# Accumulations of the modulation rows tied behind the latest low part of the weights in VectorE's order

## The chip, the cores and the metric

The kernel runs on one core of one Trainium2 chip. The metric is the device time of one execution in microseconds, less is better. A core has TensorE (PE, matrix products), VectorE (DVE), ScalarE (ACT), GpSimd (POOL) and SyncE (SP), which here issues most of the loads; each has its own queue of instructions.

## The reference, cut to what matters

One decoder layer on 512 tokens of width 2048, in float32. A vector `c` gives six modulation rows; a normalised and modulated input goes through one wide projection, whose columns feed eight heads of dilated attention and eight heads of a gated linear recurrence; then an output projection and a squared-ReLU MLP.

```python
mod = silu(c) @ w_ada + b_ada                      # 2048 x 12288
shift1, scale1, gate1, shift2, scale2, gate2 = split(mod, 6)
h = rms_norm(x, norm1_w) * (1 + scale1) + shift1
proj = h @ w_in                                    # 2048 x 7168
aq, ak, av, gq, gf, gi, gg = split(proj)
attn = rms_norm(dilated_attention(rope(norm(aq)), rope(norm(ak)), av))
hg = rms_norm(hgrn2(gq, gf, gi)) * silu(gg)        # 8 heads, 128 channels each
x = x + gate1 * (concat(attn, hg) @ w_out)
h2 = rms_norm(x, norm2_w) * (1 + scale2) + shift2
out = x + gate2 * (square(relu(h2 @ w_ff1)) @ w_ff2)
```

## The kernel before, in words

**Weights in two parts.** Every weight tile is loaded in float32 (`wraw`, 512 KB for two tiles of 128 rows, four buffers, line 192) and split by `_split` (lines 35 to 41): ScalarE casts the high part `whi` (line 39), VectorE subtracts it from the weight to get the low part `wlo` (line 40). TensorE then takes three products per block of tokens: high by high, low by high, high by low (lines 201 to 203, and 209 to 211 where channels lie on the partitions). Both parts have four buffers, so ScalarE can cast a tile only once TensorE is done with the tile four back.

**Modulation on VectorE.** A row of the modulation is a product of a vector with a 2048-row matrix. `gemv` loads 128 rows of 512 columns at a time (`araw`, 256 KB, four buffers, line 125) and VectorE multiplies and adds them into two accumulators `acc` (line 129 for the first of each, line 131 for the others). `to_cols` adds the two (line 145), TensorE transposes the sum into a bank `pc` (line 151) and ScalarE adds over the partitions (line 154). With `early` the generator belongs to the head of the program; the others, in a list `later`, are the shift's part of the columns 4608 to 5119 of the projection (the second half of the forget gates, summed with `s1c`), gate1, scale2 and shift2, and gate2 during the output projection (summed with `sc`).

**What sets the order.** A projection steps the `later` generators by 1.85 steps for every 128 rows, between its own products; the heads' generators are stepped in the same loop. Weight loads and splits are written under high priority, so that they may run ahead. TensorE's order from line 849 on is written out as the program calls it. On VectorE, ScalarE and SP the framework's scheduler picks the order from priorities and its own estimate of times; each engine then runs its list strictly in that order.

**The recurrent heads.** For each of eight heads VectorE forms nine levels of a tile `z` (lines 607 to 617; `z` of line 609 takes the keys, of line 610 the queries, `Sx` and `f` are running products), and TensorE visits them five times: pA (levels 1, 2 and 4), pB, pC, pD (level 128, line 670) and pE. Results of pA and pB come back to VectorE through masks `mt` (line 624), `near` and `AT` (line 656). The queries of the attention are normalised by `qk_norm`: VectorE line 214, a power on GpSimd (line 215), and VectorE line 433, a factor.

## Time and profile before

| what | value |
|---|---|
| runs | 2276.13, 2276.0, 2270.74 us; median 2276.0 |
| the profiled execution | 2273.58 us, of it span 2271.7 |
| granted TensorE clock, mean | 0.997 |
| VectorE: accumulations (line 131) | 392 times, 252.9 us |
| VectorE: low parts (line 40) | 368 times, 242.7 us |
| loads of `araw` | 384 of 256 KB, 4.3 us from issue to landing |
| loads of `wraw` of the projection | 104 of 512 KB, 4.2 us |

In the rows of the profile stand the line, the engine, the operation and the tiles written and read; "<-" in brackets names what ended the idle time before. The time of a matmul is modelled; from the start of one 128x512 product to that of the next it is 0.227 us where nothing waits. The program lies in three stretches: up to 100 us modulation and the first weights, then projection and heads, and from about 1030 us on the MLP, in which no accumulation of the modulation is left.

### The profile page before, as it was taken

What the parts mean: (1) busy time and instruction counts of PE and PEld (TensorE: products, weight loads), DVE (VectorE), ACT (ScalarE), POOL (GpSimd) and SP (SyncE); (2) the same over time, 40 slices, a digit from 0 to 9 for tenths busy, and PEclk for the clock granted to TensorE, in tenths of its full rate; (3) what the DMA queues carried; (4) which work ended last, traced back from release to release, by engine and by line L of the source; (5) the groups of instructions that cost most, each with busy time, mean ns of one, the idle gap of its engine ahead of it and who ended that gap; (6) DMA issues with size and microseconds to landing.
All of it is one profiled execution on the core that took longest, in us unless ns stands there. A gap on an engine that the chain in (4) does not pass through costs nothing.

```text
span 2271.7 us, 33093 instructions
## 1 busy us (share of the span) xinstructions
PE 2212.9 (97%) x11769; PEld 1822.9 (80%) x11769; DVE 1808.1 (80%) x2765; ACT 1098.1 (48%) x1950; POOL 451.6 (20%) x664
## 2 busy tenths in 40 slices
PE   4899999999999999999999999999999999999999
PEld 3788887888778888888887888888888888888887
DVE  6999878678786575678658988998897779967878
ACT  5555444434354564457545555565564333443332
POOL 1000022000230000003232323323232222222221
PEclk9999999999999999999999999999999999999999
DMA  9799455646555266837879789889889987998884
GB/s 325 254 334 336 140 177 156 217 148 204 169 166 176 67 225 205 274 115 269 317 285 360 277 303 385 297 292 369 326 293 372 359 316 258 348 348 311 306 294 163
DMA packets 262582, 598.31 MB, mean 263 GB/s; under 512 B 23220, under 2 KB 43968, under 8 KB 262416
## 3 DMA queue, kind: packets, MB, share of 16 engines
q1 hardware_dynamic: 186800, 332.54, 43.5%
q0 software_dynamic: 70720, 254.21, 30.3%
q10 hardware_dynamic: 4896, 9.44, 1.2%
q8 instruction: 93, 1.52, 0.3%
q14 instruction: 73, 0.60, 0.1%
HBM read 518.49 MB, written 77.61 MB: 262 GB/s over the span
## 4 chain that ended last, share of the span: by engine, by line
PE 69%; DVE 11%; DMA 10%; issue 6%; POOL 2%; ACT 2%; SPq 0%; DVEq 0%; POOLq 0%; ACTq 0%
PE f L1196 10%; PE f L1197 10%; PE f L1195 10%; PE prj L201 7%; PE prj L202 6%; PE prj L203 6%; DMA araw<-in_w_ada_dram 4%; PE f L211 2%; PE f L209 2%; PE f L210 2%; DVE vlo L1180 2%; DMA f_lod<-fs 2%; DVE acc L131 2%; PE prj L210 2%; PE prj L209 2%
## 5 line engine op out<-in xcount | busy, mean ns | idle before, releaser
L1179 ACT CAST vhi<-raw 128x1024 fp32r<-128x1024 f32 x392 | 413.4, 1055 | 534.6 <-PE f L1197 416.1
L1180 DVE TENSOR_TENSOR vlo<-raw,vhi 128x1024 fp32r<-128x1024 f32 x392 | 475.8, 1219 | 151.7 <-ACT vhi L1179 151.0
L1196 PE MATMUL f<-vlo,Fh 128*128 128x512 f32 x1376 | 537.0, 390 | 3.4 <-DVE vlo L1180 3.3
L1197 PE MATMUL f<-vhi,Fl 128*128 128x512 f32 x1376 | 535.6, 389 | 1.3 <-DMA Fl<-f_lod 1.3
L1195 PE MATMUL f<-vhi,Fh 128*128 128x512 f32 x1376 | 536.0, 390 | 0.0
L39 ACT CAST whi<-wraw 128x512 fp32r<-128x512 f32 (+1 forms) x368 | 219.9, 601 | 434.9 <-PE prj L203 275.8
L201 PE MATMUL prj<-whi,hi 128*128 128x512 f32 x896 | 360.5, 402 | 2.0 <-ACT gg L711 1.3
L202 PE MATMUL prj<-wlo,hi 128*128 128x512 f32 x896 | 350.6, 391 | 2.1 <-DVE wlo L40 2.1
L203 PE MATMUL prj<-whi,lo 128*128 128x512 f32 x896 | 350.9, 392 | 0.0
L131 DVE SCALAR_TENSOR_TENSOR acc<-araw,sc,acc 128x512 f32<-128x512 f32 (+1 forms) x392 | 252.9, 672 | 102.7 <-DMA araw<-in_w_ada_dram 101.4
L40 DVE TENSOR_TENSOR wlo<-wraw,whi 128x512 fp32r<-128x512 f32 (+1 forms) x368 | 242.7, 665 | 111.3 <-ACT whi L39 108.8
L1196 PEld LDWEIGHTS f<-vlo,Fh 128*128 128x128 f32 x1376 | 258.3, 188 | 61.7 <-DVE vlo L1180 8.6
L1197 PEld LDWEIGHTS f<-vhi,Fl 128*128 128x128 f32 x1376 | 258.4, 188 | 55.0 <-DMA Fl<-f_lod 1.7
L1195 PEld LDWEIGHTS f<-vhi,Fh 128*128 128x128 f32 x1376 | 258.3, 188 | 53.7 <-issue 0.3
L1163 DVE TENSOR_TENSOR raw<-raw,raw 128x1024 f32<-128x1024 f32 x224 | 268.0, 1216 | 3.8 <-DMA raw<-in_w_ff_dram 3.3
L201 PEld LDWEIGHTS prj<-whi,hi 128*128 128x128 f32 x896 | 168.8, 188 | 37.7 <-ACT gg L711 2.1
L202 PEld LDWEIGHTS prj<-wlo,hi 128*128 128x128 f32 x896 | 168.9, 188 | 36.9 <-DVE wlo L40 4.2
L203 PEld LDWEIGHTS prj<-whi,lo 128*128 128x128 f32 x896 | 168.6, 188 | 36.6 <-DVE lo L243 0.3
L1141 POOL DMA_DIRECT2D Fh<-f_hid x112 | 79.0, 705 | 421.6 <-PE f L1197 403.0
L211 PE MATMUL f<-hi,wlo 128*128 128x512 f32 x256 | 100.0, 390 | 1.5 <-DVE wlo L40 1.5
L209 PE MATMUL f<-hi,whi 128*128 128x512 f32 x256 | 100.3, 392 | 0.0
L210 PE MATMUL f<-lo,whi 128*128 128x512 f32 x256 | 99.6, 389 | 0.0
(311 smaller groups left out, 2911.2 us busy)
## 6 DMA issues: line engine op xcount, KB each, us to landing
raw<-in_w_ff_dram SPq DMA_DIRECT2D x224, 512.0 KB, 10.3
araw<-in_w_ada_dram SPq DMA_DIRECT2D x384, 256.0 KB, 4.3
Fh<-f_hid POOLq DMA_DIRECT2D x112, 512.0 KB, 6.6
Fl<-f_lod POOLq DMA_DIRECT2D x112, 512.0 KB, 7.9
wraw<-in_w_in_dram SPq DMA_DIRECT2D x104, 512.0 KB, 4.2
Fh<-h_hid POOLq DMA_DIRECT2D x60, 512.0 KB, 5.8
Fl<-h_lod POOLq DMA_DIRECT2D x60, 512.0 KB, 7.0
f_hid<-part POOLq DMA_DIRECT2D x48, 512.0 KB, 8.0
```

Source lines behind the costliest of these rows:

```text
L39: nc.scalar.copy(hi, src)
L40: (eng or nc.vector).tensor_tensor(lo, src, hi.bitcast(F32), op=ALU.subtract)
L131: dve.scalar_tensor_tensor(acc, raw[:, k - k0], vec[:, k:k + 1], acc, op0=ALU.mult, op1=ALU.add)
L201: pe.matmul(banks[ti], lhsT=hi[:, ts], rhs=whi, start=first, stop=False)
L202: pe.matmul(banks[ti], lhsT=hi[:, ts], rhs=wlo, start=False, stop=False)
L203: pe.matmul(banks[ti], lhsT=lo[:, ts], rhs=whi, start=False, stop=last)
L1163: dve.tensor_tensor(dst, a, b, op=ALU.subtract)
L1179: cast_done.append(act.copy(hi, src))
L1180: split_done.append(dve.tensor_tensor(lo, src, hi.bitcast(F32), op=ALU.subtract))
L1195: pe.matmul(banks[t], lhsT=fh[u][a][:, ts], rhs=whi[:, a], start=first, stop=False)
L1196: pe.matmul(banks[t], lhsT=fh[u][a][:, ts], rhs=wlo[:, a], start=False, stop=False)
L1197: pe.matmul(banks[t], lhsT=fl[u][a][:, ts], rhs=whi[:, a], start=False, stop=end)
```

## The change

`_split` keeps the latest subtraction that was written, and every accumulation of a `gemv` that is not `early` is written under an edge to it. The edge orders the two on VectorE's queue; it is no semaphore and no engine waits longer for it than its queue asks.

```diff
@@ _split
-    (eng or nc.vector).tensor_tensor(lo, src, hi.bitcast(F32), op=ALU.subtract)
+    _split.low = (eng or nc.vector).tensor_tensor(lo, src, hi.bitcast(F32), op=ALU.subtract)
@@ gemv
                 acc = accs[k % 2]
-                if k < 2:
-                    dve.tensor_scalar(acc, raw[:, k - k0], vec[:, k:k + 1], None, op0=ALU.mult)
-                else:
-                    dve.scalar_tensor_tensor(acc, raw[:, k - k0], vec[:, k:k + 1], acc, op0=ALU.mult, op1=ALU.add)
+                with ExitStack() if early else tc.issue_after(_split.low.ins):
+                    if k < 2:
+                        dve.tensor_scalar(acc, raw[:, k - k0], vec[:, k:k + 1], None, op0=ALU.mult)
+                    else:
+                        dve.scalar_tensor_tensor(acc, raw[:, k - k0], vec[:, k:k + 1], acc, op0=ALU.mult, op1=ALU.add)
```

The same instructions are issued on every engine. Lines below 127 have a number one higher in the changed kernel (L132 there is L131 here). VectorE's order differs from about 135 us to the output projection, SP's in the loads that go with it, TensorE's only in about 30 places ahead of the first head.

First place, VectorE in the first recurrent head, about 240 us: the low parts `wlo`, the query activations `gq` (line 764) and the levels `z_2574` and `z_2607`, which with `z_2551` feed the visit pA. Before:

```order
L764 SCALAR_TENSOR_TENSOR gq_1302<-gq_1302,scol_2484,sg_2500 128x512
L761 TENSOR_SCALAR scol_2484<-scol_2484 128x1
L617 TENSOR_TENSOR f_1292<-f_1292 128x256
L764 SCALAR_TENSOR_TENSOR gq_2095<-gq_2095,scol_2484,sg_2504 128x512
L40 TENSOR_TENSOR wlo_2709<-wraw_2706,whi_2708 128x512
L610 TENSOR_TENSOR z_2574<-gq_1300,f_1292 128x128x2
L616 TENSOR_TENSOR Sx_2549<-Sx_2549,f_1292 128x128x2
L764 SCALAR_TENSOR_TENSOR gq_2097<-gq_2097,scol_2484,sg_2508 128x512
L617 TENSOR_TENSOR f_1292<-f_1292 128x128x2
L609 TENSOR_TENSOR z_2607<-kk_2547,Sx_2549 128x64x4
L40 TENSOR_TENSOR wlo_2713<-wraw_2706,whi_2712 128x512
L610 TENSOR_TENSOR z_2607<-gq_1300,f_1292 128x64x4
```

With the change, from `wlo_2592` on:

```order
L40 TENSOR_TENSOR wlo_2592<-wraw_2585,whi_2591 128x512
L132 SCALAR_TENSOR_TENSOR acc_2558<-araw_2612,s1c_112,acc_2558 128x512
L132 SCALAR_TENSOR_TENSOR acc_2557<-araw_2615,s1c_112,acc_2557 128x512
L762 TENSOR_SCALAR scol_2484<-scol_2484 128x1 x3
L132 SCALAR_TENSOR_TENSOR acc_2558<-araw_2700,s1c_112,acc_2558 128x512
L132 SCALAR_TENSOR_TENSOR acc_2557<-araw_2703,s1c_112,acc_2557 128x512
L765 SCALAR_TENSOR_TENSOR gq_1300<-gq_1300,scol_2484,sg_2496 128x512
L765 SCALAR_TENSOR_TENSOR gq_1302<-gq_1302,scol_2484,sg_2500 128x512
L762 TENSOR_SCALAR scol_2484<-scol_2484 128x1
L40 TENSOR_TENSOR wlo_2709<-wraw_2706,whi_2708 128x512
```

then `z_2551` (line 610), an activation `gq`, `wlo_2713`, two accumulations, an `f` and an activation `gq`, and:

```order
L40 TENSOR_TENSOR wlo_2772<-wraw_2769,whi_2771 128x512
L132 SCALAR_TENSOR_TENSOR acc_2558<-araw_2763,s1c_112,acc_2558 128x512
L132 SCALAR_TENSOR_TENSOR acc_2557<-araw_2766,s1c_112,acc_2557 128x512
L611 TENSOR_TENSOR z_2574<-gq_1300,f_1292 128x128x2
L617 TENSOR_TENSOR Sx_2549<-Sx_2549,f_1292 128x128x2
L40 TENSOR_TENSOR wlo_2776<-wraw_2769,whi_2775 128x512
L132 SCALAR_TENSOR_TENSOR acc_2558<-araw_2829,s1c_112,acc_2558 128x512
L132 SCALAR_TENSOR_TENSOR acc_2557<-araw_2857,s1c_112,acc_2557 128x512
L618 TENSOR_TENSOR f_1292<-f_1292 128x128x2
L610 TENSOR_TENSOR z_2607<-kk_2547,Sx_2549 128x64x4
L132 SCALAR_TENSOR_TENSOR acc_2558<-araw_2860,s1c_112,acc_2558 128x512
L611 TENSOR_TENSOR z_2607<-gq_1300,f_1292 128x64x4
```

The accumulations of `acc_2557` and `acc_2558` stood far ahead of this place before, in rows of 138 to 208 us; eleven of them now stand between `wlo_2592` and the end of `z_2607`.

Second place, VectorE at the third projection of the heads, about 366 us: accumulations `acc_4126` and `acc_4127` of one modulation block, and the low parts `wlo_4137` and `wlo_4141`. Before:

```order
L131 SCALAR_TENSOR_TENSOR acc_4126<-araw_4409,sc_86,acc_4126 128x512
L617 TENSOR_TENSOR f_1298<-f_1298 128x64x4
L609 TENSOR_TENSOR z_4244<-kk_4091,Sx_4093 128x32x8
L40 TENSOR_TENSOR wlo_4137<-wraw_4134,whi_4136 128x512
L131 SCALAR_TENSOR_TENSOR acc_4127<-araw_4457,sc_86,acc_4127 128x512
L131 SCALAR_TENSOR_TENSOR acc_4126<-araw_4460,sc_86,acc_4126 128x512
L610 TENSOR_TENSOR z_4244<-gq_2097,f_1298 128x32x8
L616 TENSOR_TENSOR Sx_4093<-Sx_4093,f_1298 128x32x8
L131 SCALAR_TENSOR_TENSOR acc_4127<-araw_4475,sc_86,acc_4127 128x512
L617 TENSOR_TENSOR f_1298<-f_1298 128x32x8
L145 TENSOR_TENSOR acc_4126<-acc_4126,acc_4127 128x512
L40 TENSOR_TENSOR wlo_4141<-wraw_4134,whi_4140 128x512
```

With the change:

```order
L40 TENSOR_TENSOR wlo_4075<-wraw_4068,whi_4074 128x512
L618 TENSOR_TENSOR f_1298<-f_1298 128x32x8
L130 TENSOR_SCALAR acc_4126<-araw_4128,sc_86 128x512
L170 TENSOR_TENSOR gcol_115<-gcol_115,bcol_84 128x4
L130 TENSOR_SCALAR acc_4127<-araw_4131,sc_86 128x512
L40 TENSOR_TENSOR wlo_4137<-wraw_4134,whi_4136 128x512
L40 TENSOR_TENSOR wlo_4141<-wraw_4134,whi_4140 128x512
L132 SCALAR_TENSOR_TENSOR acc_4126<-araw_4161,sc_86,acc_4126 128x512
L132 SCALAR_TENSOR_TENSOR acc_4127<-araw_4164,sc_86,acc_4127 128x512
```

The whole block but its first two products now stands behind `wlo_4141`; before, its sum (line 145) stood ahead of it.

Third place, VectorE in the sixth head, about 584 us: the factor of `qk_norm` (line 433, `rs0_6312`), which waits for GpSimd's power, and the level `z_6502`, which feeds pD. Before:

```order
L616 TENSOR_TENSOR Sx_6149<-Sx_6149,f_2089 128x4x64
L40 TENSOR_TENSOR wlo_6520<-wraw_6513,whi_6519 128x512
L617 TENSOR_TENSOR f_2089<-f_2089 128x4x64
L433 TENSOR_SCALAR rs0_6312<-rs0_6312 128x16
L40 TENSOR_TENSOR wlo_6587<-wraw_6584,whi_6586 128x512
L624 TENSOR_TENSOR mt_6494<-pB_6438,hgm_107 128x128
L609 TENSOR_TENSOR z_6502<-kk_6147,Sx_6149 128x2x128
L610 TENSOR_TENSOR z_6502<-gq_5072,f_2089 128x2x128
```

With the change:

```order
L610 TENSOR_TENSOR z_6471<-kk_6147,Sx_6149 128x4x64
L434 TENSOR_SCALAR rs0_6312<-rs0_6312 128x16
L146 TENSOR_TENSOR acc_6053<-acc_6053,acc_6054 128x512
L40 TENSOR_TENSOR wlo_6587<-wraw_6584,whi_6586 128x512
L611 TENSOR_TENSOR z_6471<-gq_5072,f_2089 128x4x64
L625 TENSOR_TENSOR mt_6494<-pB_6438,hgm_107 128x128 x2
L617 TENSOR_TENSOR Sx_6149<-Sx_6149,f_2089 128x4x64
L654 TENSOR_TENSOR near_6150<-near_6150,mt_6494 128x128
L618 TENSOR_TENSOR f_2089<-f_2089 128x4x64
L610 TENSOR_TENSOR z_6502<-kk_6147,Sx_6149 128x2x128
L657 TENSOR_TENSOR AT1_459<-near_6150,mt_6494 32x4x32 x4
L611 TENSOR_TENSOR z_6502<-gq_5072,f_2089 128x2x128
```

Line 433 (434) has moved up by half a level, and ten rows instead of four now stand between it and the end of `z_6502`.

## The prediction

> **What bounds the kernel now.** I read the page's busy times first, then the windows of 50 us, then what TensorE waited for, and last the timelines around those waits.

> ```profile
> span 2271.7 us, 33093 instructions
> PE 2212.9 (97%) x11769; PEld 1822.9 (80%) x11769; DVE 1808.1 (80%) x2765; ACT 1098.1 (48%) x1950; POOL 451.6 (20%) x664
> ```

> TensorE is busy for 97% of the span, so an edit that adds and removes no instruction can win only the idle 58.8 us (2271.7 less 2212.9). The windows tell where these lie (columns: stretch, its length, busy time and count of each engine, granted clock, DMA share, GB/s).

> ```profile
> 0.00:50.00 50.00, 20.08 (x108) 16.75 (x109) 31.61 (x84) 27.17 (x67) 9.63 (x24) 1.00 0.98 323
> 50.00:100.00 50.00, 42.17 (x180) 32.86 (x180) 50.00 (x127) 26.77 (x62) 0.00 (x0) 0.93 0.96 317
> 150.00:200.00 50.00, 49.99 (x223) 40.64 (x222) 50.00 (x88) 26.97 (x60) 0.53 (x1) 1.00 1.03 371
> 200.00:250.00 50.00, 49.46 (x346) 40.58 (x345) 46.77 (x93) 27.43 (x62) 0.00 (x0) 1.00 0.68 223
> 350.00:400.00 50.00, 48.98 (x439) 40.09 (x438) 39.66 (x87) 20.67 (x58) 9.47 (x12) 1.00 0.59 180
> 550.00:600.00 50.00, 46.45 (x421) 38.20 (x420) 39.37 (x93) 19.79 (x71) 16.59 (x26) 0.97 0.52 160
> ```

> The first 100 us hold 37.7 of the 58.8 (29.9 and 7.8), before the order of any engine differs. From 100 us on 21 us are left in all. Between 100 and 1030 us, where the tied accumulations run, TensorE waited for:

> ```profile
> PE pD L670 <- DVE z L610: 3.4, 2, 2.9
> PE prj L202 <- DVE wlo L40: 2.1, 3, 0.7
> PE f L211 <- DVE wlo L40: 1.5, 2, 0.9
> PE prj L201 <- ACT gg L711: 1.3, 1, 1.3
> PE prj L201 <- ACT whi L39: 0.6, 2, 0.3
> PE pB L583 <- DVE z L610: 0.6, 1, 0.6
> PE pc L151 <- DVE acc L145: 0.5, 1, 0.5
> ```

> That is 10.0 us. Two rows are not VectorE's late low parts or z: `gg` (1.3), and `f L211` (1.5), a projection of the MLP. The target is 7.2 us: one wait of 2.9 and a handful of 0.3 to 0.7.

> **What makes a low part late.** VectorE is 80% busy and takes its queue in order. Around 367 us (start, length, engine, line, operation, names, in brackets the idle time before):

> ```profile
> 364.87 0.75 DVE L131 SCALAR_TENSOR_TENSOR acc<-araw,sc,acc 128x512 f32<-128x512 f32 x1 [0.41 <-DMA araw<-in_w_ada_dram]
> 365.54 0.42 DVE L617 TENSOR_TENSOR f<-f 128x256 f32<-128x256 f32 x1
> 365.88 0.69 DVE L145 TENSOR_TENSOR acc<-acc 128x512 f32<-128x512 f32 x1
> 366.48 0.68 DVE L40 TENSOR_TENSOR wlo<-wraw,whi 128x512 fp32r<-128x512 f32 x1
> ...
> 367.22 0.50 PE L202 MATMUL prj<-wlo,hi 128*128 128x512 f32 x1 [0.72 <-DVE wlo L40]
> ```

> The low part did not wait for its high part; it stood behind accumulations, one of which waited for its load. TensorE started 0.06 us after the low part's end.

> **Term 1, the small waits: 3.7 us won.** In the order rows of the second place four accumulations (0.67 apart) and a sum (0.6) stood ahead of `wlo_4141`, 3.3 us; now two plain products (0.41 each) do, 2.5 us less for a wait of 0.72. The other small waits (the row of `prj L202`, that of `pB`, the lesser of the two `pD` waits, the sum `pc`) have the same make-up. Their sum is 2.1 + 0.6 + 0.5 + 0.5 = 3.7. Bounds: nothing, if the accumulations that stay ahead wait for loads as the one at 364.87 did, and 4.3 with the two waits on whi.

> **Term 2, the long wait at 586 us: 2.2 won, between 0 and 4.5.**

> ```profile
> 573.68 0.75 DVE L131 SCALAR_TENSOR_TENSOR acc<-araw,sc,acc 128x512 f32<-128x512 f32 x1 [2.00 <-DMA araw<-in_w_ada_dram]
> ...
> 577.96 0.17 DVE L214 TENSOR_SCALAR rs<-rs 128x16 f32<-128x16 f32 x1
> ...
> 584.48 0.17 DVE L433 TENSOR_SCALAR rs<-rs 128x16 f32<-128x16 f32 x1 [2.81 <-POOL rs L215]
> ...
> 585.70 0.42 DVE L610 TENSOR_TENSOR z<-gq,f 128x256 f32<-128x256 f32 x1
> ...
> 578.21 6.24 POOL L215 TENSOR_TENSOR rs<-rs,mhalf 128x16 f32<-128x16 f32 x1 [4.38 <-DVE rs L214]
> ...
> 586.26 0.68 PE L670 MATMUL pD<-z 128*128 128x128 f32 x4 [2.87 <-DVE z L610]
> ...
> 588.28 0.63 PE L202 MATMUL prj<-wlo,hi 128*128 128x512 f32 x1
> 588.71 0.63 PE L203 MATMUL prj<-whi,lo 128*128 128x512 f32 x1
> ```

> Here no accumulation is the last cause: L433 waited 2.81 us for GpSimd's power, and the z for pD stood behind L433. After the wait eight matmuls started 0.43 us apart, where the usual distance is 0.227: 8 x 0.2 = 1.6 us more, which makes the place worth 2.9 + 1.6 = 4.5. The change starts the chain earlier: the masks and L214 stood behind an accumulation that waited 2.00 us for a load, and now lie behind a low part with the accumulations after it. Against it, two accumulations (1.3 us) come between that low part and L214, and behind L433 now stand ten rows up to the end of the z: a sum and a low part (0.6 each), seven of 0.2 to 0.34 (1.9) and the four AT (1.2), with the last z 0.4, in all 4.8 us, where 1.6 stood (584.48 to 586.12). With a power of 6.24 us the z ends 11.3 us behind L214 (0.25 + 6.24 + 4.8); TensorE wants it at 583.39, so L214 must start by 572.1, 5.9 us earlier than now, for the wait to vanish. It gains the 2.00 and some of the accumulations' work ahead. I take half of the place, 2.2.

> Another run of the same power took

> ```profile
> 296.47 3.49 POOL L215 TENSOR_TENSOR rs<-rs,mhalf 128x16 f32<-128x16 f32 x1 [0.78 <-DVE rs L214]
> ```

> beside a VectorE that was just as full, so 3 us of the 6.24 may be chance. [...]

> **Term 3, the first head: 4.0 us lost, with a slow clock 5.6.** The order rows of the first place speak against the change. Before, 14 accumulations of the fifth shift group ran far ahead, at 138 to 208 us, in pairs like these:

> ```profile
> 176.69 1.40 DVE L131 SCALAR_TENSOR_TENSOR acc<-araw,s1c,acc 128x512 f32<-128x512 f32 x2
> 178.01 1.40 DVE L131 SCALAR_TENSOR_TENSOR acc<-araw,sc,acc 128x512 f32<-128x512 f32 x2
> ```

> A pair takes 1.33 us, one 0.67. Tied, they stand at 230 to 262 us, 11 of them between `wlo_2592` and the end of `z_2607`, which TensorE's first visit pA needs. The timelines of VectorE and TensorE there:

> ```profile
> 235.53 0.69 DVE L40 TENSOR_TENSOR wlo<-wraw,whi 128x512 fp32r<-128x512 f32 x1 [0.69 <-ACT whi L39]
> ...
> 238.13 0.74 DVE L764 SCALAR_TENSOR_TENSOR gq<-gq,scol,sg 128x512 f32<-128x512 f32 x1
> ...
> 243.06 0.42 DVE L610 TENSOR_TENSOR z<-gq,f 128x256 f32<-128x256 f32 x1
> 243.40 0.42 DVE L616 TENSOR_TENSOR Sx<-Sx,f 128x256 f32<-128x256 f32 x1
> ...
> 246.40 0.46 PE L583 MATMUL pA<-gq,kk 128*32 128x32 f32 x32
> 246.68 1.05 PE L583 MATMUL pA<-z 128*32 128x32 f32 x96
> ```

> The low part at 235.53 starts when its high part is cast, and these casts follow TensorE, so it can't come earlier. From its start VectorE has, by the new order: five low parts at 0.60 (3.0), 11 accumulations at 0.67 (7.3), four L764 at 0.67 (2.7), four short L761 at 0.08 (0.3), seven of z, Sx and f at 0.34 (2.3). Sum 15.6: the z ends at 251.2, where it ended at 243.48. The last third of pA's 96 matmuls starts at about 247.2 (246.68 and two thirds of its 0.8). So TensorE waits 4.0 us where it had 3.7 to spare. The eight slow matmuls of 588 us followed an idle stretch of 2.87, so another 1.6 is likely. I take 5.0, between 4.0 and 5.6.

> [...]

> **Smaller terms.** At 387 us the new order puts a sum and a low part's followers ahead of the last z for pD:

> ```profile
> 383.50 1.28 DVE L40 TENSOR_TENSOR wlo<-wraw,whi 128x512 fp32r<-128x512 f32 x2
> ...
> 385.24 0.41 DVE L610 TENSOR_TENSOR z<-gq,f 128x256 f32<-128x256 f32 x1
> ...
> 387.05 0.49 PE L670 MATMUL pD<-z 128*128 128x128 f32 x2
> ```

> The second low part starts at 384.10; behind it come itself and the sum (0.6 each), four of 0.34 and three of 0.2, then the z ends: 3.2 us later, 387.3 against 387.05. With the same at one more head I take 0.8 lost, between 0 and 2.5. The sums L145 for the transposes pc come later in the new order; TensorE waited for such a sum only once, 0.5 us, with the next work of its group far off, so I take nothing, and a late one would cost its lateness once. A wait of 1.43 us for a stage-2 low part at 1266 us sits where a VectorE row or two also moved: 0.7 won, between 0 and 1.4.

> **Sum.** -3.7 - 2.2 + 5.0 + 0.8 - 0.7 = -0.8 us. The profiled execution took 2273.58 us (span 2271.7 and 1.9 around it), so 2272.8; the median of the runs shown, 2276.0, lies 2.4 above that execution. I predict 2275.

> **The rivals.**

> *All waits cured, nothing new* (faster). The sum would be -3.7 - 4.5 - 1.4 = -9.6: 2266. For it: every low part from 140 to 970 us has less VectorE work ahead than before. Against it: term 3, which is a plain count of rows. It needs z_2607 on time, 7.7 us earlier than counted.

> *The ties make VectorE wait for loads in front of the z* (slower). The place is the first head again. The accumulation loads have four buffers, so a pair's load starts when the pair two ahead is done, and lands late:

> ```profile
> araw<-in_w_ada_dram SPq DMA_DIRECT2D x384, 256.0 KB, 4.3
> DVE acc L131 <- DMA araw<-in_w_ada_dram: 98.7, 72, 5.5
> ```

> With 4.3 to land, 0.7 for two issues and 1.33 for the pair, two pairs take 6.3 us or 3.2 each; my count spaces them 2.8 apart, so 0.4 x 5 = 2 us more. On SP's queue these loads now also stand behind weight loads that wait for a buffer; if each of five pairs waits 2.0 us, as at 573.68, the first head costs 5.6 + 10 = 15.6, terms 1 and 2 shrink to 3.7, and the time is +12 or 2288. It decides from 1.0 us a pair (5.6 + 5 x 1.0 - 3.7 is the 6.8 of the bound below). Against it: SP reached the loads of 236 to 262 us early before.

> *Term 3 absorbed, all else as summed*: -5.8, 2270, still within 0.3% of the median.

> **How the numbers follow.** The measurement tells 0.3% (6.8 us) from no change. The forecast, with its own range of 2269 to 2281 (the bounds above, -7 to +5), has 0.50; the absorbed term 3 has 0.13, three quarters of it inside 0.3%; the full cure 0.20, mostly below 2269.2; the waits for loads 0.17, nearly all above 2282.8. With the edges of the forecast, faster 0.24, same 0.59, slower 0.17, and the range that leaves out 2 in 10 is 2265 to 2284.

> **What would show it.** Term 1: the rows `prj L202 <- wlo` and `pc <- acc` gone or under 1 us in all. Term 2: the wait for L433 under 2.8 and the 550 to 600 window above 46.45. Term 3: a wait of pA for z at about 247 us, which no row shows now, with slow matmuls after it. If pA doesn't wait, the forecast is wrong toward faster; if the accumulations ahead of `z_2607` show idle time for araw, toward slower.

## The result

| kernel | median, us | lowest to highest | ratio to before, 95% interval |
|---|---|---|---|
| before | 2275.97 (11 runs) | 2270.74 to 2277.51 | |
| with the ties | 2270.97 (11 runs) | 2268.63 to 2273.67 | 0.998, 0.997 to 0.9989 |

The change wins 5.0 us, 0.22%: the interval of the ratio leaves out 1, and the gain is inside the 0.3% that was called no change. The forecast was 2275 in 2265 to 2284. Its place and sign of each large term were right; the sum was 4 us too slow. The profiled execution of the changed kernel took 2268.98 us, 4.6 less than that of before. In the changed kernel's profile all lines below 127 have a number one higher. Its totals and what TensorE waited for from 100 to 1030 us:

```profile
span 2267.1 us, 33088 instructions
PE 2212.1 (98%) x11769; PEld 1824.7 (80%) x11769; DVE 1808.9 (80%) x2765; ACT 1097.5 (48%) x1950; POOL 439.1 (19%) x664
```

```profile
PE pA L584 <- DVE z L611: 4.4, 2, 3.5
PE pho L692 <- ACT far_sb L684: 1.9, 2, 1.0
PE prj L202 <- ACT gg L712: 1.7, 2, 1.3
PE f L212 <- DVE wlo L40: 1.0, 2, 0.8
PE pD L671 <- DVE z L611: 0.9, 1, 0.9
```

The busy times of TensorE, VectorE and ScalarE changed by less than 1 us (GpSimd's fell by 12.5, from 451.6); TensorE waits elsewhere. All rows of before for projection low parts, for pB and for pc are gone, pD fell from 3.4 to 0.9, and a wait of 4.4 at pA is new, as term 3 said. What VectorE waited for turned round in the same stretch:

```profile
DVE wlo L40 <- ACT whi L39: 139.1, 97, 5.9
DVE acc L132 <- DMA araw<-in_w_ada_dram: 19.9, 22, 2.5
```

Before, accumulations waited 98.7 us for loads with low parts behind them; now low parts wait for their high part, which costs nobody anything, and most loads have landed by the time an accumulation's turn comes.

**Where the time went.** For each stretch I compared the start of the same matmul in both traces, counted from the span's start (negative: the changed kernel is earlier); below this is called matched matmuls. The sum at a time, and what each step added (rounded; drifts of 0.1 to 0.2 between the steps are left out):

| us of before | step, us | changed kernel earlier or later, us | what stands there |
|---|---|---|---|
| to 225 | -1.2 | -1.2 | the first 100 us, -0.6, and a step of -0.6 at 200 |
| 235 | -0.8 | -2.0 | wait of pc for a sum gone |
| 245 to 260 | +7.0 | +5.0 | pA, first head |
| 300 to 360 | +1.5 | +6.5 | new waits of pD and of pho (less the lesser wait of pD, gone) |
| 367 | -1.6 | +4.9 | wait for wlo gone |
| 577 | -1.2 | +3.5 | wait for wlo gone |
| 586 to 591 | -4.5 | -1.0 | pD and the slow matmuls gone |
| 620 to 655 | -1.3 | -2.3 | pB and wlo gone (-2.3), new wait of pho (+1.0) |
| to 1240 | -0.5 | -2.8 | small steps of both signs |
| 1250 to 1270 | -1.1 | -3.9 | wait of 1.4 for a stage-2 low part gone |
| to the end | -0.3 | -4.2 | |

**The first head.** VectorE and TensorE in the changed kernel around the new wait:

```profile
234.32 0.69 DVE L40 TENSOR_TENSOR wlo<-wraw,whi 128x512 fp32r<-128x512 f32 x1 [2.52 <-ACT whi L39]
234.93 1.41 DVE L132 SCALAR_TENSOR_TENSOR acc<-araw,s1c,acc 128x512 f32<-128x512 f32 x2
...
249.54 0.42 DVE L611 TENSOR_TENSOR z<-gq,f 128x256 f32<-128x256 f32 x1
...
244.44 0.46 PE L584 MATMUL pA<-gq,kk 128*32 128x32 f32 x32
244.72 0.49 PE L584 MATMUL pA<-z 128*32 128x32 f32 x32
246.08 0.46 PE L584 MATMUL pA<-z 128*32 128x32 f32 x32 [0.87 <-DVE z L611]
250.02 0.66 PE L584 MATMUL pA<-z 128*32 128x32 f32 x32 [3.48 <-DVE z L611]
250.60 0.80 PE L202 MATMUL prj<-whi,hi 128*128 128x512 f32 x1
251.20 0.63 PE L203 MATMUL prj<-wlo,hi 128*128 128x512 f32 x1
...
254.61 0.60 PE L202 MATMUL prj<-whi,hi 128*128 128x512 f32 x1
```

From the start of that low part to the end of the z are 249.96 - 234.32 = 15.6 us, the number that the count of rows gave. None of the accumulations between waited for a load. Behind the wait stand ten matmuls about 0.43 us apart.

**586 us.** The factor (line 434) waits 0.2 us instead of 2.81, and the last z ends 0.2 us before pD:

```profile
576.85 0.29 DVE L215 TENSOR_SCALAR rs<-rs 128x16 f32<-128x16 f32 x1
...
581.80 0.17 DVE L434 TENSOR_SCALAR rs<-rs 128x16 f32<-128x16 f32 x1 [0.18 <-POOL rs L216]
...
586.22 0.42 DVE L611 TENSOR_TENSOR z<-gq,f 128x256 f32<-128x256 f32 x1
...
578.81 2.95 POOL L216 TENSOR_TENSOR rs<-rs,mhalf 128x16 f32<-128x16 f32 x1
...
586.81 0.71 PE L671 MATMUL pD<-z 128*128 128x128 f32 x4
```

The way from L434 to the end of the z is 4.8 us, as counted; the power took 2.95 us instead of 6.24.

### The profile page after: what moved, and what is told of

The parts are those of the page before. It is cut to its first block, busy times and chain, and to the rows that moved or that the text cites. A ratio compares the mean times of both kernels' runs of the same rounds, so it can differ in the third digit from the quotient of the medians.

```text
span 2267.1 us, 33088 instructions
## 1 busy us (share of the span) xinstructions
PE 2212.1 (98%) x11769; PEld 1824.7 (80%) x11769; DVE 1808.9 (80%) x2765; ACT 1097.5 (48%) x1950; POOL 439.1 (19%) x664
## 4 chain that ended last, share of the span: by engine, by line
PE 67%; issue 12%; DMA 9%; DVE 8%; POOL 3%; ACT 1%; SPq 0%; POOLq 0%; DVEq 0%; ACTq 0%
PE f L1198 8%; PE f L1197 8%; PE f L1196 8%; PE prj L202 8%; PE prj L204 8%; PE prj L203 8%; DMA f_lod<-fs 2%; PE f L212 2%; PE f L210 2%; PE f L211 2%; PE prj L211 2%; PE prj L212 2%; PE prj L210 2%; DVE vlo L1181 2%; DMA Fl<-h_lod 2%
## 5 line engine op out<-in xcount | busy, mean ns | idle before, releaser
L39 ACT CAST whi<-wraw 128x512 fp32r<-128x512 f32 (+1 forms) x368 | 220.7, 602 | 464.8 <-PE prj L204 330.9
L40 DVE TENSOR_TENSOR wlo<-wraw,whi 128x512 fp32r<-128x512 f32 (+1 forms) x368 | 245.7, 671 | 181.8 <-ACT whi L39 170.5
L202 PE MATMUL prj<-whi,hi 128*128 128x512 f32 x896 | 360.7, 403 | 1.8 <-ACT gg L712 1.7
L203 PE MATMUL prj<-wlo,hi 128*128 128x512 f32 x896 | 349.8, 390 | 0.0
L132 DVE SCALAR_TENSOR_TENSOR acc<-araw,sc,acc 128x512 f32<-128x512 f32 (+1 forms) x392 | 250.4, 677 | 22.9 <-DMA araw<-in_w_ada_dram 22.2
L202 PEld LDWEIGHTS prj<-whi,hi 128*128 128x128 f32 x896 | 168.9, 189 | 36.6 <-ACT gg L712 2.9
L203 PEld LDWEIGHTS prj<-wlo,hi 128*128 128x128 f32 x896 | 169.1, 189 | 32.7
L211 PE MATMUL f<-lo,whi 128*128 128x512 f32 x256 | 99.6, 389 | 0.0
## 6 DMA issues: line engine op xcount, KB each, us to landing
araw<-in_w_ada_dram SPq DMA_DIRECT2D x384, 256.0 KB, 4.6
```

The lines of the kernel that those rows point to most:

```text
L39: nc.scalar.copy(hi, src)
L40: _split.low = (eng or nc.vector).tensor_tensor(lo, src, hi.bitcast(F32), op=ALU.subtract)
L132: dve.scalar_tensor_tensor(acc, raw[:, k - k0], vec[:, k:k + 1], acc, op0=ALU.mult, op1=ALU.add)
L202: pe.matmul(banks[ti], lhsT=hi[:, ts], rhs=whi, start=first, stop=False)
L203: pe.matmul(banks[ti], lhsT=hi[:, ts], rhs=wlo, start=False, stop=False)
```

## The experiments

Before took 2273.33 to 2274.71 us as a median beside these runs and 2275.97 in the result, so each kernel is read by its ratio to before on its own chip.

| kernel | median, us | before there | ratio, 95% interval |
|---|---|---|---|
| the change, again | 2270.95 | 2273.58 | 0.9988, 0.9979 to 0.9996 |
| the change, shift group free | 2267.31 and 2267.34 | 2273.89 and 2273.58 | 0.9969, 0.9958 to 0.9979; 0.9975, 0.9964 to 0.9985 |
| ties in the shift group alone | 2279.07 and 2279.66 | 2273.89 and 2274.71 | 1.0019, 1.001 to 1.0028; 1.0016, 1.0005 to 1.0027 |
| shift group tied from the sixth accumulation | 2267.71 | 2273.58 | 0.9974, 0.9965 to 0.9984 |
| before, factor on GpSimd | 2269.4 | 2273.89 | 0.9987, 0.9978 to 0.9996 |
| shift group free, factor on GpSimd | 2266.55 | 2273.58 | 0.9967, 0.9955 to 0.9979 |
| ties in gate2 alone | 2274.5 | 2274.71 | 0.9999, 0.9991 to 1.0008 |
| shift group free, ties one pair looser | 2263.94 | 2274.71 | 0.9956, 0.9943 to 0.997 |
| shift group free, ties two pairs looser | 2263.28 | 2273.33 | 0.996, 0.9945 to 0.9975 |

### Is the loss in the first head the fifth shift group's?

```diff
-                with ExitStack() if early else tc.issue_after(_split.low.ins):
+                with ExitStack() if early or view is win_v else tc.issue_after(_split.low.ins):
```

> The change, but the fifth shift group (the accumulations of columns 4608 to 5119) is left untied; its accumulations then stand where they stood before, ahead of wlo_2592, and all other groups stay tied. Theory (the ties win in the later heads and lose in the first one, by a count of rows): TensorE's wait of 4.4 us for z at pA (246 to 250 us) and the ten slow matmuls after it vanish; this head cost 7.0 us against before, so the median falls from 2271.0 to about 2264. Rival (the wait only takes the place of later ones: TensorE, earlier by 7 us, catches VectorE again at the next heads): new waits for z or wlo between 300 and 700 us, and 2268 to 2271. Second rival (the hoisted accumulations fill VectorE at 150 to 200 us and delay pc): the 0.5 us wait of pc for acc L145 at 235 us comes back, 2265 to 2266.

Measured: 2267.31, ratio 0.9969. The wait at pA and the slow matmuls are gone:

```profile
PE pho L692 <- ACT far_sb L684: 1.9, 2, 1.0
PE prj L202 <- ACT gg L712: 1.7, 2, 1.3
PE f L212 <- DVE wlo L40: 1.0, 2, 0.8
PE pD L671 <- DVE z L611: 0.9, 1, 0.9
```

No new wait for z or wlo stands between 300 and 700 us: the first rival falls, and so does the second, since pc does not wait either. By matched matmuls this kernel is 0.5 us earlier than before at 310 us, where the changed kernel is 5.9 later: 6.4 us given back. But the median fell by less than the expected 7, so I ran both on one chip.

> The changed kernel, unchanged, beside the others of this call, so that differences of 2 to 7 us are read on one chip. Theory: 5.0 us under before again (ratio 0.998), with the wait of 4.4 us at pA in its profile.

> The change without ties in the fifth shift group, a second time beside the changed kernel itself. Theory: the first head gives back 6.4 us, as its first profile showed between 240 and 300 us, so 6 us under the changed kernel where the MLP runs alike. Rival: later waits, in the MLP above all, take part of it, and it is 2.5 us under, as the two ratios (0.998 and 0.9969) say.

Measured: 2270.95 and 2267.34, 3.6 us apart, between theory and rival; the ratio of the change to before was 0.9988 here, 0.998 at first, with overlapping intervals. The profile of the change repeated its wait at pA (4.3 us). Of the 6 us given back by 750 us, the MLP takes part. Neither profile of the changed kernel has the wait of 1.4 us for a stage-2 low part that before had at 1266 us; in the first profile of the free kernel it is there again:

```profile
1258.20 0.50 PE L1197 MATMUL f<-vlo,Fh 128*128 128x512 f32 x1 [1.52 <-DVE vlo L1181]
```

VectorE's order in the MLP differs between the two kernels in a few places (so much the orders show), though no tie reaches that far. The second profile of the free kernel has no such wait (longest 0.5), but there TensorE lost 2.7 us between 750 and 1000 and 3.0 near 1237, where the first gained 0.5 and lost 0.2. At both places it waited, 1.8 us for a low part and 2.0 us for an `s` of VectorE. The second profile of before lost 3.0 near 1237 in the same way. So this part differs from one execution to the next, and no run fixes it.

The opposite, ties on the shift group alone:

> Before, with the ties on the fifth shift group alone. Theory: the first head pays 4.4 us of waiting at pA and about 2 us of slow clock, the later waits (wlo at 367, 577 and 652 us, z at 586 us) stay as they were: 2276 plus 6 to 7, about 2282, and the wait at pA starts when eleven accumulations have passed, 15.6 us after the start of wlo_2592. Rival (the loss in the first head is taken out again by slack behind it): 2276 to 2278.

> Before, with the ties on the fifth shift group alone, a second time for its profile. Theory: a wait of 4.3 to 4.4 us at pA and slow matmuls behind it, TensorE 6.9 us later across 240 to 260 us than before, and the waits of before at 345 to 652 us behind it; 5 to 7 us over before. Rival: the later waits shrink by what TensorE lost, and it ends within 2 us of before.

Measured: 2279.07 and 2279.66, ratios 1.0019 and 1.0016: slower by 4 to 5 us (the profile is that of the second run; in the first it fell on an execution of 5777 us, the only one of its kind). The first head costs what it cost in the changed kernel, 7.0 us:

```profile
PE pA L584 <- DVE z L611: 4.3, 2, 3.5
PE pD L671 <- DVE z L611: 2.9, 1, 2.9
PE prj L203 <- DVE wlo L40: 2.8, 4, 1.0
```

and the large waits of before stand behind it. It is less than 7 in the sum because the ties win 1.4 us ahead of the head (200 and 235 us), and because this time no slow matmuls followed the wait at 586 us (last section).

### Is the wait a count of rows?

```diff
+                with ExitStack() if early or (view is win_v and k < 5) else tc.issue_after(_split.low.ins):
```

> The change, but of the fifth shift group only the accumulations from the sixth on are tied. Eight instead of eleven then stand between wlo_2592 and the end of z_2607: 13.7 us of rows instead of 15.6. Theory (the count of rows is the wait): TensorE waits 2.3 to 2.5 us at pA instead of 4.4. If ten slow matmuls follow again, the head gets 2.0 us better than the changed kernel's, if none follow, 4.0. Rival (the accumulations wait for their loads there): the wait stays above 3.5, with idle time of acc for araw.

Measured: 2267.71, ratio 0.9974, and

```profile
PE pA L584 <- DVE z L611: 2.5, 1, 2.5
```

```profile
235.29 0.69 DVE L40 TENSOR_TENSOR wlo<-wraw,whi 128x512 fp32r<-128x512 f32 x1 [2.51 <-ACT whi L39]
...
248.52 0.41 DVE L611 TENSOR_TENSOR z<-gq,f 128x256 f32<-128x256 f32 x1
```

248.93 - 235.29 = 13.6 us, where 13.7 were counted. Three accumulations less are 2.0 us less, and the wait fell from 4.4 to 2.5. Slow matmuls followed again, 0.43 us apart (from 250.81 us on); the head cost 4.3 us instead of 7.0. No accumulation waited for its load: the rival of loads has no place here. The median, though, does not follow the heads alone: on the same chip the free kernel took 2267.34, the same, while its profile has TensorE 4.5 us earlier at 760 us. The losses in the MLP told of above take that up in this pair of profiles; for the medians no run shows where it goes.

### What made the long wait at 586 us?

```diff
         if i == 0:
-            dve.tensor_scalar(rv, rv, QS, None, op0=ALU.mult)
+            pool.tensor_scalar(rv, rv, QS, None, op0=ALU.mult)
```

> Before, with the factor of the query norm (L433) moved from VectorE to GpSimd, behind its power; no ties. VectorE then never waits for the power. Theory (the wait of 2.9 us at 586 us comes from VectorE's queue standing behind L433 and recurs in every execution): the wait for z at pD and the eight slow matmuls go, 2276 minus 4.5, about 2271.5. Rival (a long power of 6.24 us is chance, and most executions have one near 3.4): within 1 us of before.

> Before, unchanged, for a second profile. Theory: the same waits again: wlo three times (0.6 to 0.8 us), z at pD about 586 us. If the power behind L214 at 578 us takes 3.4 us instead of 6.24, the wait at 586 us is under 0.5 us, and the 3 us between executions of before (2270.7 to 2277.5) are this place; rival: the wait is there again with a power of about 6 us.

Measured: 2269.4 with the factor on GpSimd, ratio 0.9987, 3.0 to 4.5 us won; by matched matmuls 4.4 us at 587. The other waits of before stayed or grew a little (low parts of the heads' projections 3.3 us in six waits, where before had 2.1 in three). The second profile of before had the wait again (pD 3.8 us in all, longest 2.9), with the same long power (first row below); and the kernel with the factor on GpSimd had a still longer one, and no wait (the other rows):

```profile
577.39 6.24 POOL L215 TENSOR_TENSOR rs<-rs,mhalf 128x16 f32<-128x16 f32 x1 [2.72 <-DVE rs L214]
```

```profile
580.58 6.83 POOL L215 TENSOR_TENSOR rs<-rs,mhalf 128x16 f32<-128x16 f32 x1 [4.41 <-DVE rs L214]
...
585.73 0.71 PE L670 MATMUL pD<-z 128*128 128x128 f32 x4
```

The kernels with ties in the shift group alone and in gate2 alone, whose order at this place is that of before, waited as long for this z, 2.88 and 2.9 us. So the long power belongs to this order and is no chance, and it was VectorE's queue behind L433 that passed it on to TensorE.

> The change without ties in the fifth shift group, and the factor of the query norm on GpSimd. Theory: VectorE no longer stands behind the power, so the wait of 0.9 us for z at pD near 303 us goes; nothing else differs from the kernel without those ties: 1 us under it, the fastest of all. Rival (GpSimd's second instruction delays the queries): a new wait for aq or z, equal or slower than it.

Measured: 2266.55, ratio 0.9967; beside 2267.34 no difference that the intervals can tell. The part of the theory about 303 us fell: the wait for z at pD stayed (1.0 us). There VectorE did not stand behind the power:

```profile
304.08 0.16 DVE L434 TENSOR_SCALAR rs<-rs 128x16 f32<-128x16 f32 x1
...
305.16 0.68 DVE L146 TENSOR_TENSOR acc<-acc 128x512 f32<-128x512 f32 x1
...
307.50 0.67 DVE L40 TENSOR_TENSOR wlo<-wraw,whi 128x512 fp32r<-128x512 f32 x1
...
309.11 0.42 DVE L611 TENSOR_TENSOR z<-gq,f 128x256 f32<-128x256 f32 x1
...
309.68 0.57 PE L671 MATMUL pD<-z 128*128 128x128 f32 x3 [0.89 <-DVE z L611]
```

(the changed kernel's timeline). It stood behind a sum and a low part that the tight ties had pushed between L434 and the z.

### Where does the gain lie, and how tight must the tie be?

```diff
+                with ExitStack() if early or view is not ada_v or col0 < 5 * D else tc.issue_after(_split.low.ins):
```

> Before, with the ties on the last group alone (gate2, during the output projection). Theory (the gain lies in the heads): the waits of before at 345 to 652 us stay, the time is that of before to within 1 us. Rival (the ties also win at the output projection or in the MLP's order): 1 to 3 us under before, with the wait for vlo at 1266 us gone.

Measured: 2274.5, ratio 0.9999. Its profile has the waits of before (wlo 3.0, pD 2.9) and the wait at 1266 us (1.4): the gain lies in the heads' groups.

```diff
-    _split.low = (eng or nc.vector).tensor_tensor(...)
+    low = (eng or nc.vector).tensor_tensor(...)
+    _split.low = (getattr(_split, "low", []) + [low])[-3:]
...
+                with ExitStack() if early or view is win_v else tc.issue_after(_split.low[-3].ins):
```

> The change without ties in the fifth shift group, and with the other ties one pair of weight tiles looser: an accumulation must stand behind the third latest low part instead of the latest. Theory (what hurts is a block of accumulations that runs far ahead; a pair more or less does not matter, since a low part's high part is cast four tiles ahead): the waits for wlo at 367, 577 and 652 us stay away, and so does the one at 586 us: the same time as with the tight ties, 2267 (ratio to before 0.997). Rival (the tie has to be to the latest): waits for wlo come back, 1 to 4 us slower than with the tight ties.

Measured: 2263.94, ratio 0.9956. That is under the tight ties with a free shift group (0.9969 and 0.9975), but the intervals overlap. No wait of the heads' projections for a low part and none for a z is left (`f` is the MLP):

```profile
PE pho L693 <- ACT far_sb L685: 1.9, 2, 1.2
PE prj L203 <- ACT gg L713: 1.3, 1, 1.3
PE f L213 <- DVE wlo L40: 0.3, 1, 0.3
```

The place of the wait at 309 us shows what the looser tie does: neither the sum nor the low part stands ahead of the z any more, and pD does not wait.

```profile
301.14 0.42 DVE L612 TENSOR_TENSOR z<-gq,f 128x256 f32<-128x256 f32 x1
301.47 0.42 DVE L618 TENSOR_TENSOR Sx<-Sx,f 128x256 f32<-128x256 f32 x1
301.81 1.17 DVE L658 TENSOR_TENSOR AT<-near,mt 32x128 f32<-32x128 f32 x4
303.00 0.69 DVE L40 TENSOR_TENSOR wlo<-wraw,whi 128x512 fp32r<-128x512 f32 x1
...
302.68 0.71 PE L672 MATMUL pD<-z 128*128 128x128 f32 x4
```

> As the kernel whose ties are one pair of weight tiles looser, with the ties two pairs looser (the fifth latest low part); the fifth shift group stays untied. Theory (a bounded run ahead is enough, and the tight tie only crowds accumulations behind the low parts in front of the z): within 2 us of the one-pair kernel, ratio to before 0.9955 to 0.9965, no wait for wlo over 0.4 us between 300 and 700 us. Rival (each pair of looseness lets a block of accumulations back in front of the low parts): the waits at 367 and 652 us come back in part, 0.997 to 0.998.

Measured: 2263.28, ratio 0.996, the same as one pair, with no wait for a low part over 0.4 us between 300 and 700 us. By matched matmuls TensorE is 11.7 us earlier than before at 760 us, where it is 9.0 with one pair and 8.2 and 8.0 with the tight ties and a free shift group; this profile lost about 4.9 of them again between 1200 and 1240 us. So a bound of some pairs on the run ahead is enough. Both loose kernels beat before, and their medians are the lowest of all; but they ran on other chips than the tight ties, the intervals overlap, and in the heads one pair shows no more than 1 us of the 2 to 4 us between the ratios.

## Why the prediction was right, and where its sizes were off

*Bounds.* Right in the main: TensorE's waits moved and the slow matmuls behind them (which count as busy time, so that the bound of idle time leaves them out), and busy times stayed within 1 us on TensorE and VectorE.

*Term 1, 3.7 us.* Right in mechanism, too small: the steps at 235, 367, 577, 620 and 650 us add up to 0.8 + 1.6 + 1.2 + 0.7 + 1.6 = 5.9. The view of waits gives the idle time alone; a wait of 0.72 at 367 moved the next matmuls by 1.0, and the wait of 0.3 just ahead of it, for a high part, went too.

*Term 2, 2.2 us between 0 and 4.5.* At its upper end, 4.5. The step that failed is the power's time: I kept 6.24 us as the likelier end, and it took 2.95. The count behind L434 (4.8 us) held, and L215 came only 1.1 us earlier (576.85 against 577.96), far from the 5.9 that a long power would have asked for. TensorE, 3.5 us late from the first head, came later too, but lateness alone wins nothing: with ties in the shift group alone TensorE is 5 us late here and waits the same 2.88 us. Without the lateness the wait is gone as well (the kernel with the free shift group, power 2.95). So it was the shorter power. The prediction called VectorE just as full beside the power of 3.49 us; beside the one of 6.24 it was idle for the last 2.8. What makes it long in the order of before, no run shows (last section).

*Term 3, 5.0 us.* The place, the count of 15.6 us and the slow clock (0.50 granted from 248.22 to 255.05 us) held. Mis-sized: 7.0 us. TensorE reached pA 2.0 us earlier than before while the low part that starts the count came only 1.2 earlier, so it lost 4.7 instead of 4.0 between matmul starts; and ten matmuls were slow, not eight, for another 2.3 instead of 1.6.

*Smaller terms.* The 0.8 us at 387 us did not come. In its place came 1.0 at 309 us (the same make-up, two heads earlier), 1.2 and 1.0 for `far_sb` on ScalarE, whose order I hadn't walked, and 0.5 at 743. The wait for a stage-2 low part at 1266 us went as hoped, 1.1 us against the first profile of before; the second profile of before had hardly any (0.5) and lost 3.0 us near 1237 instead, so its size is not fixed.

*Sum.* By the steps of the table: -5.9 - 4.5 + 7.0 on the three terms, +3.1 on new small waits (less the pD of 345), -1.1 in the MLP, the rest about -2.8, of which the 0.6 of the first 100 us is no effect of the change: a second profile of before was 0.9 earlier there. In all -4.2 where -0.8 stood. No large term was closer than 2 us: two were won by 2.2 and 2.3 more than forecast, one lost 2.0 more, and that these partly cancel was luck.

*Rivals.* The measured 2271 lies next to the 2270 of the rival in which term 3 is absorbed; its mechanism was wrong all the same, for term 3 was paid in full and other terms won more. The full cure did not happen in the change, but exists: the kernels with loose ties are at 0.9956 and 0.996, 9 to 10 us, where 9.6 was worked out. It asked for less than the prediction said: z_2607 had to end 4.0 us earlier than counted, when TensorE comes to it, not 7.7. The accumulations in front of the z never waited for their loads, so the rival of loads was wrong in its premise: with the accumulations later, their loads had landed.

## What to carry to other kernels

An edge that holds background work back does not remove the work; look where it lands, count the rows ahead of the next instruction that the bounding engine waits for, and leave free what used idle time before. A bound on how far background work may run ahead need not be tight: the tight one packs the work right behind each foreground piece, in front of the next (the 0.9 us at 309 us), and the loose ones were at least as fast. A count of rows from an anchor that the bounding engine itself paces was good to 0.1 us in two kernels; sums of idle time were a third too small.

## What the runs showed of the hardware

**Half clock after a wait.** The slow matmuls do not follow every wait of a size. Before, an idle 2.87 us at 586 us was followed by eight matmuls at 0.43 us. In the kernel with ties on the shift group alone the same wait, 2.88 us, was followed by none:

```profile
591.65 0.68 PE L671 MATMUL pD<-z 128*128 128x128 f32 x4 [2.88 <-DVE z L611]
592.09 0.47 PE L202 MATMUL prj<-whi,hi 128*128 128x512 f32 x1
592.40 0.39 PE L203 MATMUL prj<-wlo,hi 128*128 128x512 f32 x1
```

```profile
583.61:587.02 3.41, 0.76 (x6) 0.74 (x6) 2.54 (x9) 0.73 (x4) 0.83 (x1) 1.00 0.25 98
587.02:590.43 3.41, 3.41 (x10) 2.63 (x9) 3.34 (x11) 0.33 (x1) 0.69 (x1) 0.50 0.00 0
586.54:589.95 3.41, 2.23 (x30) 1.58 (x28) 0.61 (x4) 1.49 (x4) 3.29 (x1) 1.00 0.52 154
589.95:593.36 3.41, 1.71 (x10) 1.53 (x11) 3.34 (x13) 0.37 (x1) 0.00 (x0) 1.00 0.00 0
```

Before, 2.65 us of the wait fell into one stretch, and the next one ran at half clock. In the other kernel the wait was shared out, 1.18 and 1.70, and neither stretch had a slow one behind it. In the traces of before and of the change, from 60 to 2255 us, the full-clock stretches that were followed by one at half clock had 1.90 and 2.65 us idle (before, 88.68 and 583.61 us) and 3.03 and 2.56 (the change, 91.21 and 244.81 us); all other full-clock stretches had 1.33 or less. So the two waits of 2.87 and 2.88 us had different prices, and what differed was how they lay on this grid.

**The power on GpSimd.** The power of 128x16 in the sixth head took 6.24 us in both profiles of before (from 578.21 and from 577.39 us on), 6.83 with the factor on GpSimd, and 2.95 in the change. The five others of this shape took 3.32 to 3.49 us in before and 2.90 to 3.02 in the change. In before, VectorE runs through nine products and differences of two tiles without a pause for the first 3.5 us of the long one (to 581.67), and then stands idle behind the factor for the last 2.8. A power beside which VectorE ran one low part of 0.69 us and nothing else took 2.90 (the change):

```profile
406.71 2.90 POOL L216 TENSOR_TENSOR hrs<-hrs,mhalf 128x16 f32<-128x16 f32 x1 [47.24 <-DVE hrs L215]
```

A busy VectorE alone does not account for the long one: at 296.47 us, beside instructions of the same sort, the power took 3.49, and in the change 2.95, with VectorE busy up to 0.14 us before its end. In the change GpSimd came to the power straight from its rotations, and before after 4.38 us of idleness; whether that decides, no run here shows.
